# Eight gate projections of a hybrid attention/SSD block: placed between the attention heads, with the gates kept in DRAM

## The chip, the cores and the metric

One core of a Trainium2 chip runs the whole program. The metric is device time in microseconds of one execution, as the median of several. TensorE (PE in the rows) multiplies matrices, VectorE (DVE) and ScalarE (ACT) work on elements, GpSimd (POOL) does a few powers, and SyncE (SP) issues nearly all DMA transfers.

## What is computed

One encoder block with two parallel branches over 16 learned rows and 512 input rows, width 1024, in float32:

```python
u = rmsnorm(h, norm_w)
proj = u @ w_in                      # latents, rope key, gate of attention, SSD z/x/B/C/dt, merge gates
y_a = mla_branch(q_lat, kv_lat, k_rope, ...)          # 16 heads
y_a = (y_a * silu(g_attn)) @ w_attn_proj
y_s = ssd_branch(z, xbc, dt_raw, ...) @ w_ssd_proj    # chunked scan, both directions, 4 groups
gates = sigmoid(merge).reshape(B, L, 2, 1024)
mixed = gates[:, :, 0] * y_a + gates[:, :, 1] * y_s
h = rmsnorm(h + mixed @ w_out, final_norm_w)
```

The change concerns `gates[:, :, 0]`, the output gate of the attention branch: eight blocks of 128 columns, each a projection of `u` (contraction 1024, 512 rows).

## The kernel before

**Arithmetic.** Every projection is done as three passes of float32r matmuls: the operands are split into a high and a low part, and high x high, high x low and low x high are summed in PSUM. A projection of 128 output columns over 512 rows is therefore 24 matmuls (8 blocks of the contraction, 3 passes). Its weights come in as one 512 KB load into `wr` (2 buffers); ScalarE casts the high part `wh` and VectorE subtracts to get the low part `wl` (3 buffers each), `weights`, lines 492 to 516.

**Stages.** First the norm of the input, then four groups of the SSD branch, each with its projections, and from about 500 us the 16 attention heads. A head is `score_gen` (four score tiles in two double-bank PSUM buffers, tag "d"; maximum on VectorE, exponential on ScalarE, normalisation) and `value_gen` (five rounds: TensorE transposes the probabilities, ScalarE and VectorE split them into `pT`, TensorE multiplies them with the values into `o`). Each pair of heads p needs projections `q_unit(p)`, `k_unit(p)`, `g_fill(p)` (the silu gate, 24 matmuls), every second pair `pe_unit` and `v_unit`. After head 15, `split_y` makes the high and low parts `yah`, `yal` of the attention output, `mix_unit(m)` for eight blocks m projects them with `w_attn_proj`, multiplies with the gate and adds the SSD part, and `out_unit` multiplies with `w_out` (tile `wo`), followed by residual and norm.

**The merge gates.** `merge_s(m)` (lines 1268 to 1278) makes the gate of the SSD branch and applies it to `ysacc` at once. `merge_a(m)` (lines 1283 to 1292) makes tanh of half the projection for the attention branch: 24 matmuls, then one ScalarE activation into a tile `ma`. That tile stays in the pool of slots until `mix_unit(m)` uses it (lines 1303 to 1319).

**Room.** One pool of `NSLOT` = 31 slots of 128 x 512 float32 holds nearly all working tiles: the latents, the values, the small weights `ws` of the heads, the heads' outputs, the gates, and at the end `yah`, `yal` (16 slots) and `mxh`, `mxl` (up to 16). PSUM has 4 single banks, tag "m", for projections, transposes and `o`.

**The order.** Nothing runs in the order in which it is written. `drive` (lines 1441 to 1460) steps through generators with a clock of its own: the `mains` (the heads, the SSD stages) and a `queue` of fillers, of which the first 20 (`LOOK`) are looked at and up to 4 (`OPEN`) are under way at a time; each has a condition on what is done. A main item that is ready goes before a filler. What is recorded so gets a rank, and `_Recorder.order` (lines 164 to 255) then lists all operations by the earliest time at which a cost table says they can go, ties by rank, on every engine and on SP. An operation that is the first to use a pool's tile may overtake at most 4 (`AHEAD`) older tiles of the same pool. The sorted list is emitted; each engine keeps its part of it.

The fillers around the change, in the queue's order for each pair p: `pe_unit`, `q_unit`, `k_unit`, `v_unit`, `merge_s(p)`, `g_fill(p + 1)` (lines 1525 to 1535). Behind all pairs come the eight `merge_a`, with one condition for all: head 13 (`GATES`) is done (line 1536). `mix_unit` is admitted when all eight `split_y` are done (line 1545).

Of the kernel before, what the change touches and what calls it, by code (L numbers as in the profile page):

```python
# [9 lines left out]
F32 = mybir.dt.float32  # L10
# [6 lines left out]
P = 128  # L17
D = 1024
NM = 16
NX = 512  # L20
# [5 lines left out]
KD = D // P  # L26
NC = NX // P
EPS = 1e-6
NH = 16
# [14 lines left out]
LAG = 1250.0  # L44
MAHEAD, TOKC, CBC = 2, 2, 1
MAINS, OPEN, LOOK = 24, 4, 20
QLATE, GATES, SPLIT = 1, 13, 99


WPOOL, WPOOLB = 2, 4  # L50
# [2 lines left out]
class _Plan:  # L53
# [7 lines left out]
    @staticmethod  # L61
    def region(ap):
        step = ap.ap[0][0]
        p0, f0 = divmod(ap.offset, step) if step else (0, ap.offset)
        span = sum(abs(st) * (n - 1) for st, n in ap.ap[1:]) + 1
        return ap.name, p0, p0 + ap.shape[0], f0, f0 + span
# [25 lines left out]
class _Recorder:  # L92
# [15 lines left out]
    @classmethod  # L108
    def region(cls, ap):
        step = ap.ap[0][0]  # L110
        if ap.name == "cum_rows":
            return 0, 1, [(0, 1)]
        p0, f0 = divmod(ap.offset, step) if step else (0, ap.offset)
        dims = [(st, n) for st, n in ap.ap[1:] if st and n > 1]
        if "PSUM" in str(getattr(ap, "space", "")):
            end = f0 + sum(st * (n - 1) for st, n in dims)
            return 0, P, [(f0 // cls.BANK * cls.BANK, (end // cls.BANK + 1) * cls.BANK)]
        dims.sort(reverse=True)
        spans = [(f0, f0 + 1)]
        for k, (st, n) in enumerate(dims):  # L120
            rest = sum(a * (b - 1) for a, b in dims[k:]) + 1
            inner = sum(a * (b - 1) for a, b in dims[k + 1:]) + 1
            if inner >= st or n * len(spans) > 32:
                return p0, p0 + ap.shape[0], [(a, a + rest) for a, _ in spans]
            spans = [(a + st * m, a + st * m + 1) for a, _ in spans for m in range(n)]
        return p0, p0 + ap.shape[0], spans
# [227 lines left out]
def hybrid_block_kernel(ctx, tc, a, out):  # L354
    nc = tc.nc
    scr = nc.dram_tensor("cum_rows", (2, NC, 32, P), F32, kind="Internal").ap()

    cp = ctx.enter_context(tc.tile_pool(name="cp", bufs=1))
    rp = ctx.enter_context(tc.tile_pool(name="rp", bufs=WRAW))
# [12 lines left out]
    def nm(s):  # L372
        uid[0] += 1
        return f"{s}_{uid[0]}"

    def slot(shape, dt=F32, name="s"):
        return rec.tile(sp.tile(shape, dt, tag="s", name=nm(name)), "s", NSLOT)
# [15 lines left out]
    def bank(tag, shape, name, wait=lambda: True):  # L393

        yield lambda: wait() and bool(banks[tag]) and done.look(min(banks[tag]))
        banks[tag].remove(min(banks[tag]))
        return (psm if tag == "m" else psd)(shape, name=name)

    def drop(tag):
        banks[tag].append(plan.unit_end)  # L400
# [17 lines left out]
    done = Done()  # L418
# [5 lines left out]
    V, A, G, T = (_Eng(plan, rec, n, e) for n, e in (("DVE", nc.vector), ("ACT", nc.scalar), ("POOL", nc.gpsimd), ("PE", nc.tensor)))  # L424
    S, Q = _Queue(plan, rec, nc.sync), _Queue(plan, rec, nc.scalar, "ACT")
# [4 lines left out]
    def tt(eng, o, x, y, op):  # L430
        eng.tensor_tensor(o, x, y, op=op)

    def lo_of(eng, lo, x, hi):
        eng.tensor_tensor(lo, x, hi.bitcast(F32), op=ALU.subtract)

    def mm(o, lhs, rhs, start=True, stop=True):
        T.matmul(o, lhsT=lhs, rhs=rhs, start=start, stop=stop)
# [54 lines left out]
    def weights(srcs, k, c, small=False):  # L492
        after = 0.0
        if small:
            raw = slot([P, k, c], name="ws")
        else:
            after = min(raws)
            raws.remove(after)
            raw = rec.tile(rp.tile([P, k, c], F32, tag="wr", name=nm("wr")), "rpwr", WRAW)
        for dst, src in srcs(raw):  # L500
            S.dma_start(dst, src, after)
        yield
        if small:
            hi, lo = slot([P, k, c], F32R, name="wsh"), slot([P, k, c], F32R, name="wsl")
        else:
            yield lambda: bool(splits) and done.look(min(splits))
            splits.remove(min(splits))
            hi = rec.tile(wp.tile([P, k, c], F32R, tag="wh", name=nm("wh")), "wpwh", WSPLIT)
            lo = rec.tile(wp.tile([P, k, c], F32R, tag="wl", name=nm("wl")), "wpwl", WSPLIT)
        wcount[0] += 1  # L510
        A.copy(hi, raw)
        lo_of(V, lo, raw, hi)
        if not small:
            raws.append(plan.unit_end)
        yield
        return hi, lo

    def wdone():
        splits.append(plan.clk["PE"] + 100.0)

    def w_cols(c0, M=P):
        return weights(lambda raw: [(raw, w_in[:, :, c0:c0 + M])], KD, M)
# [3 lines left out]
    def proj(w, src, cols, M=P, tag="m", width=HALF):  # L526


        hi, lo = w
        n = len(src)  # L530
        parts = [cols] if tag == "m" else cols
        ps = yield from bank(tag, [P, 512] if tag == "m" else [P, 2, 512], "pj", lambda: not mid[0])
        seq = [(hi, 0, k) for k in range(n)] + [(lo, 0, k) for k in range(n)] + [(hi, 1, k) for k in range(n)]
        for h, s in list(enumerate(parts))[::-1]:
            o = ps[:M, :cols.stop - cols.start] if tag == "m" else ps[:M, h, :width]
            for i, (x, y, k) in enumerate(seq):
                mm(o, x[:, k, :], src[k][y][:, s], start=(i == 0), stop=(i == len(seq) - 1))
                mid[0] = h > 0 or i < len(seq) - 1
                if i % (PART * len(parts)) == PART * len(parts) - 1 and mid[0]:
                    yield  # L540
        return o if tag == "m" else ps[:M, :, :width]
# [256 lines left out]
    def has(*keys):  # L798
        return lambda: all(k in done for k in keys)
# [318 lines left out]
    def score_ok(h):  # L1118
        return h < 0 or ("S", h) in done
# [148 lines left out]
    def merge_s(m):  # L1268
        w = yield from w_cols(O_MS + m * P)
        ps = yield from proj(w, u_src, QRY)  # L1270
        wdone()
        yield
        z = slot([P, NX], name="ms")
        A.activation(z, ps, AF.Tanh, scale=0.5)
        drop("m")
        yield
        V.scalar_tensor_tensor(ysacc[:, m, :], z, 1.0, ysacc[:, m, :], op0=ALU.add, op1=ALU.mult)
        done.add(("ms", m))

    w_ap = a["w_attn_proj"][0].rearrange("(k p) m -> p k m", p=P)  # L1280
    mx_, gates, ysp = {}, {}, {}

    def merge_a(m):
        w = yield from w_cols(O_MA + m * P)
        ps = yield from proj(w, u_src, QRY)
        wdone()
        yield
        z = slot([P, NX], name="ma")
        A.activation(z, ps, AF.Tanh, scale=0.5)
        drop("m")  # L1290
        gates[m] = z
        done.add(("ga", m))

    def split_y(p):
# [7 lines left out]

    def mix_unit(m):
        w = yield from weights(lambda raw: [(raw, w_ap[:, :, m * P:(m + 1) * P])], KD, P)
        ps = yield from proj(w, [ysp[p] for p in range(KD)], slice(0, NX))
        wdone()
        yield has(("ga", m), ("ms", m))
        z = gates.pop(m)
        V.scalar_tensor_tensor(z, z, 1.0, ps, op0=ALU.add, op1=ALU.mult)
        drop("m")  # L1310
        tt(V, z, z, ysacc[:, m, :], ALU.add)
        yield
        h = slot([P, NX], F32R, name="mxh")
        l = slot([P, NX], F32R, name="mxl")
        A.copy(h, z)
        yield
        lo_of(V, l, z, h)
        mx_[m] = (h, l)
        done.add(("mx", m))
# [117 lines left out]
    def fill(makes, cond=None):  # L1437
        for mk in makes:
            queue.append(Item(mk, cond))
# [31 lines left out]
    def proj_fill(g):  # L1471
        fill([mark(lambda m=m: proj_unit(g, m), ("proj", g, m)) for m in range(4)], lambda: epi_ok(g))
# [52 lines left out]
    for p in range(KD):  # L1525
        if p % 2 == 0:
            fill([lambda p=p: pe_unit(p // 2)], lambda p=p: lat_ok() and score_ok(2 * p - 3))
        fill([lambda p=p: q_unit(p), lambda p=p: k_unit(p)], lambda p=p: "att" in done and lat_ok() and score_ok(2 * p - 2))
        if p % 2 == 0:
            fill([lambda p=p: v_unit(p // 2)], lambda p=p: lat_ok() and (p == 0 or ("A", 2 * p - 3) in done))  # L1530
        if p == 0:
            proj_fill(3)
        fill([lambda p=p: merge_s(p)], lambda p=p: ("proj", 3, p // 2) in done)
        if p + 1 < KD:
            g_fill(p + 1)
    fill([lambda m=m: merge_a(m) for m in range(KD)], lambda: ("A", GATES) in done)
    for h in range(NH):
        main(lambda h=h: score_gen(h), lambda h=h: ("q", h) in done and ("k", h) in done
             and (h < 1 or ("P", h - 1) in done) and (h < 2 or ("A", h - 2) in done))
# [47 lines left out]
```

## Time and profile before

| | |
|---|---|
| median of 3 runs | 912.46 us (910.71 to 915.15) |
| the profiled execution, its own time | 913.33 us |
| its span, first to last instruction | 911.5 us |
| TensorE busy | 878.5 us (96%) |
| VectorE busy | 707.9 us (78%) |
| ScalarE busy | 543.2 us (60%) |
| granted TensorE clock, mean | 0.996 |
| DMA | 83.30 MB, 91 GB/s |

"Busy" is the union of an engine's records. A record of a matmul lasts from its start to its modelled end (about 0.39 us for 512 columns), while the next one starts 0.23 us later, so that short stalls do not show as idle time. Row formats: `out<-in` names the tiles written and read, `x` is a count, and in brackets stands idle time of the engine just ahead of the instruction with what ended it. All operations are recorded at line 261, where the sorted list is emitted, so the rows are told apart by tile names: `pj<-uh,wh` (and `wl`, `ul`) is a projection of `u` in 512-column matmuls, `pj<-nh,wsh` one of the latents, `sc` the scores, `pt` the transposes, `o` the value products, `v` the values, `pj<-yah,wh` a mix projection, `wo` the output.

### The profile page before, as it was taken

What the parts mean: (1) busy time and instruction counts of PE and PEld (TensorE: products, weight loads), DVE (VectorE), ACT (ScalarE), POOL (GpSimd) and SP (SyncE); (2) the same over time, 40 slices, a digit from 0 to 9 for tenths busy, and PEclk for the clock granted to TensorE, in tenths of its full rate; (3) what the DMA queues carried; (4) which work ended last, traced back from release to release, by engine and by line L of the source; (5) the groups of instructions that cost most, each with busy time, mean ns of one, the idle gap of its engine ahead of it and who ended that gap; (6) DMA issues with size and microseconds to landing.
All of it is one profiled execution on the core that took longest, in us unless ns stands there. A gap on an engine that the chain in (4) does not pass through costs nothing.

```text
span 911.5 us, 13243 instructions
## 1 busy us (share of the span) xinstructions
PE 878.5 (96%) x4984; PEld 725.7 (80%) x4984; DVE 707.9 (78%) x1245; ACT 543.2 (60%) x1159; POOL 11.7 (1%) x20
## 2 busy tenths in 40 slices
PE   7999999999989999999999999999999999999997
PEld 5997878867878769977788888877777878888885
DVE  6798799968799689979768757969989897334464
ACT  6369469965776447855344556757777685432232
POOL 1000000000000000000001000000000000000000
PEclk9999999999999999999999999999999999999998
DMA  7254246434524236332224333121121001433322
GB/s 219 71 165 119 70 120 166 109 93 113 141 70 139 70 84 160 104 116 70 70 70 102 81 87 92 38 53 29 38 50 33 15 24 47 135 121 101 104 70 92
DMA packets 126952, 83.30 MB, mean 91 GB/s; under 512 B 26354, under 2 KB 114071, under 8 KB 126889
## 3 DMA queue, kind: packets, MB, share of 16 engines
q1 hardware_dynamic: 126709, 82.33, 33.3%
q8 instruction: 39, 0.64, 0.3%
q14 instruction: 24, 0.20, 0.1%
q10 hardware_dynamic: 180, 0.14, 0.0%
HBM read 80.22 MB, written 2.23 MB: 90 GB/s over the span
## 4 chain that ended last, share of the span: by engine, by line
PE 74%; DVE 17%; ACT 4%; issue 2%; DMA 1%; POOL 0%; POOLq 0%; ACTq 0%; DVEq 0%
PE pj L261 53%; PE wo L261 4%; PE sc L261 3%; PE st L261 2%; PE yo L261 2%; PE o L261 2%; DVE x L261 2%; DVE wl L261 2%; PE pt L261 2%; PE tr L261 2%; PE yd L261 1%; DVE mx L261 1%; DVE pT L261 1%; DVE yo L261 1%; DVE C L261 1%
## 5 line engine op out<-in xcount | busy, mean ns | idle before, releaser
L261 PE MATMUL pj<-uh,wh 128*128 128x512 f32 (+3 forms) x776 | 158.8, 346 | 8.0 <-DVE yo L261 3.5
L261 DVE TENSOR_TENSOR wl<-wr,wh 128x1024 fp32r<-128x1024 f32 (+1 forms) x102 | 123.9, 1217 | 53.2 <-ACT wh L261 53.0
L261 PE MATMUL pj<-uh,wl 128*128 128x270 f32 (+3 forms) x776 | 157.1, 339 | 0.0
L261 PE MATMUL pj<-ul,wh 128*128 128x270 f32 (+3 forms) x776 | 150.0, 335 | 0.0
L261 ACT CAST wh<-wr 128x1024 fp32r<-128x1024 f32 (+1 forms) x102 | 106.3, 1042 | 63.1 <-PE pj L261 41.3
L261 PEld LDWEIGHTS pj<-uh,wh 128*128 128x128 f32 (+1 forms) x776 | 121.9, 191 | 27.6 <-issue 5.1
L261 PEld LDWEIGHTS pj<-ul,wh 128*128 128x128 f32 (+1 forms) x776 | 122.6, 189 | 15.0
L261 PEld LDWEIGHTS pj<-uh,wl 128*128 128x128 f32 (+1 forms) x776 | 122.0, 190 | 13.2 <-issue 0.2
L261 ACT ACTIVATE ar<-ar,nacs 128x128 f32<-128x128 f32 x256 | 80.8, 391 | 24.5 <-DMA ar<-cum_rows 19.3
L261 PE MATMUL sc<-kst,qst 96*128 96x264 f32 (+1 forms) x384 | 67.2, 299 | 6.3 <-ACT p L261 5.4
L261 PEld LDWEIGHTS sc<-kst,qst 96*128 96x128 f32 (+1 forms) x384 | 53.6, 189 | 11.7 <-ACT p L261 8.6
L261 ACT ACTIVATE p<-sc,mx 128x528 f32<-128x528 f32 x64 | 45.3, 707 | 21.3 <-DVE mx L261 20.8
L261 PE MATMUL pt<-cst,p 128*128 128x128 f32 (+1 forms) x320 | 52.2, 274 | 1.4 <-DVE pT L261 0.8
L261 DVE TENSOR_TENSOR pT<-pt,pT 128x512 fp32r<-128x512 f32 x64 | 43.8, 685 | 11.5 <-ACT pT L261 11.3
L261 PE MATMUL o<-pT,v 128*128 128x512 f32 x128 | 46.6, 417 | 3.5 <-ACT pT L261 2.9
L261 DVE SCALAR_TENSOR_TENSOR x<-pj,chv,x 128x528 f32<-128x528 f32 x64 | 48.8, 763 | 0.8 <-ACT x L261 0.3
L261 PEld LDWEIGHTS pt<-cst,p 128*128 128x128 f32 (+1 forms) x320 | 37.3, 130 | 12.7 <-DVE p L261 1.5
L261 DVE TENSOR_REDUCE mx<-sc 128x1 f32<-128x528 f32 x64 | 44.6, 698 | 2.2 <-PE sc L261 1.9
L261 ACT CAST pT<-pt 128x512 fp32r<-128x512 f32 x64 | 37.3, 587 | 14.6 <-PE pt L261 14.4
L261 ACT ACTIVATE w<-cbm,dt_t 128x128 f32<-128x128 f32 x128 | 39.9, 390 | 2.9 <-DVE cbm L261 2.9
L261 PE MATMUL pj<-nh,wh 128*128 128x512 f32 x128 | 39.6, 431 | 0.0
L261 DVE SCALAR_TENSOR_TENSOR w<-cbm,dt_t,w 128x128 f32<-128x128 f32 x128 | 38.1, 347 | 0.0
(224 smaller groups left out, 1467.2 us busy)
## 6 DMA issues: line engine op xcount, KB each, us to landing
wr<-in_w_in SPq DMA_DIRECT2D x69, 512.0 KB, 4.0
ar<-cum_rows SPq DMA_DIRECT2D x32, 512.0 KB, 5.3
wr<-in_w_ssd_proj SPq DMA_DIRECT2D x16, 512.0 KB, 3.4
wr<-in_w_attn_proj SPq DMA_DIRECT2D x8, 512.0 KB, 3.6
wr<-in_w_out SPq DMA_DIRECT2D x8, 512.0 KB, 3.7
ws<-in_w_uq SPq DMA_DIRECT2D x36, 64.0 KB, 3.3
xt<-in_x SPq DMA_DIRECT2D x4, 512.0 KB, 5.3
fin<-in_x SPq DMA_DIRECT2D x4, 512.0 KB, 6.0
```

What stands on the lines that cost most here:

```text
L261: o.fn(*o.args, **o.kw)
```

## The change

`merge_a(m)` no longer keeps its tile for the mix: it stores the 256 KB of tanh to a DRAM tensor `gate_rows`, and `mix_unit(m)` loads them into a new slot, after its weights and ahead of its projection. The queue has `merge_a(p - 1)` right behind `merge_s(p)`, admitted when head 2p - 1 is done (for p = 1 to 7), and `merge_a(7)` behind all pairs, admitted when head 14 is done. The recorder treats each block of the new tensor as a region of its own, so that a load depends on its own store alone. The arithmetic is the same.

```diff
-QLATE, GATES, SPLIT = 1, 13, 99
+QLATE, SPLIT = 1, 99
@@
             return 0, 1, [(0, 1)]
+        if ap.name == "gate_rows":
+            return 0, 1, [(ap.offset // (P * NX), ap.offset // (P * NX) + 1)]
@@
     scr = nc.dram_tensor("cum_rows", (2, NC, 32, P), F32, kind="Internal").ap()
+    gate_scr = nc.dram_tensor("gate_rows", (KD, P, NX), F32, kind="Internal").ap()
@@
-    mx_, gates, ysp = {}, {}, {}
+    mx_, ysp = {}, {}
@@ def merge_a(m):
         z = slot([P, NX], name="ma")
         A.activation(z, ps, AF.Tanh, scale=0.5)
         drop("m")
-        gates[m] = z
+        yield
+        S.dma_start(gate_scr[m], z)
         done.add(("ga", m))
@@ def mix_unit(m):
         w = yield from weights(lambda raw: [(raw, w_ap[:, :, m * P:(m + 1) * P])], KD, P)
+        yield has(("ga", m))
+        z = slot([P, NX], name="ga")
+        S.dma_start(z, gate_scr[m])
         ps = yield from proj(w, [ysp[p] for p in range(KD)], slice(0, NX))
         wdone()
-        yield has(("ga", m), ("ms", m))
-        z = gates.pop(m)
+        yield has(("ms", m))
         V.scalar_tensor_tensor(z, z, 1.0, ps, op0=ALU.add, op1=ALU.mult)
@@
         fill([lambda p=p: merge_s(p)], lambda p=p: ("proj", 3, p // 2) in done)
+        if p:
+            fill([lambda p=p: merge_a(p - 1)], lambda p=p: ("A", 2 * p - 1) in done)
         if p + 1 < KD:
             g_fill(p + 1)
-    fill([lambda m=m: merge_a(m) for m in range(KD)], lambda: ("A", GATES) in done)
+    fill([lambda: merge_a(KD - 1)], lambda: ("A", NH - 2) in done)
```

## Rows read from the trace of the kernel before

**Rows 1.** The page: busy time of each engine.
```profile
PE 878.5 (96%) x4984; PEld 725.7 (80%) x4984; DVE 707.9 (78%) x1245; ACT 543.2 (60%) x1159; POOL 11.7 (1%) x20
```
**Rows 2.** Busy us of each engine (instructions in brackets), and granted clock, in four stretches.
```profile
core 0: us, PE busy (x) PEld busy (x) DVE busy (x) ACT busy (x) POOL busy (x), PEclk, DMA share, GB/s
...
615.70:762.80 147.10, 137.45 (x835) 114.78 (x835) 131.02 (x267) 109.00 (x234) 0.00 (x0) 1.00 0.14 32
763.40:815.80 52.40, 52.40 (x254) 42.97 (x253) 23.22 (x33) 21.60 (x36) 0.00 (x0) 1.00 0.39 118
815.80:877.00 61.20, 61.20 (x266) 49.60 (x265) 26.42 (x32) 16.29 (x19) 0.00 (x0) 1.00 0.28 88
577.70:615.70 38.00, 37.23 (x230) 31.66 (x228) 29.42 (x61) 24.77 (x56) 0.00 (x0) 1.00 0.25 58
```
**Rows 3.** TensorE's timeline among the gates: start, duration, matmuls in a run.
```profile
768.21 0.60 PE L261 MATMUL pt<-cst,p 128*128 128x128 f32 x4
768.57 2.08 PE L261 MATMUL pj<-uh,wh 128*128 128x512 f32 x8
...
780.20 0.89 PE L261 MATMUL sc<-kst,qst 128*128 128x264 f32 x6
780.93 1.08 PE L261 MATMUL pj<-uh,wl 128*128 128x512 f32 x4
...
804.65 2.02 PE L261 MATMUL pj<-uh,wh 128*128 128x512 f32 x8
806.51 2.01 PE L261 MATMUL pj<-uh,wl 128*128 128x512 f32 x8
```
**Rows 4.** TensorE's groups by shape, 615.7 to 762.8 us: first and last.
```profile
L261 PE MATMUL o<-pT,v 128*128 128x512 f32 x80 | 30.3, 421 | 3.3 <-ACT pT L261 2.9 <-DVE pT L261 0.4
...
L261 PE MATMUL v<-wsh,nl 128*16 128x256 f32 x4 | 0.8, 278 | 0.0
```
**Rows 5.** TensorE's groups by shape, 577.7 to 615.7 us: first and last.
```profile
L261 PE MATMUL pt<-cst,p 128*128 128x128 f32 x39 | 6.5, 275 | 0.3 <-DVE p L261 0.3
...
L261 PE MATMUL v<-wsh,nh 128*16 128x256 f32 x2 | 0.4, 279 | 0.0
```
**Rows 6.** TensorE's groups by shape, 763.4 to 815.8 us: first and third.
```profile
L261 PE MATMUL pj<-uh,wl 128*128 128x512 f32 x64 | 17.3, 398 | 0.0
...
L261 PE MATMUL pj<-uh,wh 128*128 128x512 f32 x56 | 14.4, 398 | 0.0
```
**Rows 7.** Who waited for whom from 560 us on: total us, times, longest.
```profile
PEld sc L261 <- ACT p L261: 8.6, 13, 1.7
...
PEld o L261 <- ACT pT L261: 3.6, 3, 1.3
```
**Rows 8.** Tile `ma`, the gates: duration ns min/median/max, first and last start us.
```profile
L261 ACT ACTIVATE ma<-pj x8: 578/598/602, 767.9 to 816.0; 128x512 f32<-128x512 f32 x8
L261 DVE SCALAR_TENSOR_TENSOR ma<-ma,pj x8: 681/689/689, 821.5 to 877.2; 128x512 f32<-128x512 f32 x8
```
**Rows 9.** Tile `wh`, 577 to 816 us: the two parts of a block of weights.
```profile
L261 ACT CAST wh<-wr x15: 1037/1049/1067, 580.0 to 810.9; 128x1024 fp32r<-128x1024 f32 x15
L261 DVE TENSOR_TENSOR wl<-wr,wh x15: 1209/1225/1227, 586.2 to 812.0; 128x1024 fp32r<-128x1024 f32 x15
```
**Rows 10.** DMA issues from 560 us on: count, size, median us to landing.
```profile
out<-fo SPq DMA_DIRECT2D x8, 256.0 KB, 2.2
...
fw<-in_final_norm_w SPq DMA_DIRECT2D x2, 256.0 KB, 4.3
```
**Rows 11.** VectorE's timeline: output sums of heads 13 and 15, and the last split.
```profile
763.57 0.69 DVE L261 TENSOR_TENSOR y<-o,y 64x512 f32<-64x512 f32 x1
...
806.99 0.69 DVE L261 TENSOR_TENSOR y<-o,y 64x512 f32<-64x512 f32 x1
...
809.09 0.69 DVE L261 TENSOR_TENSOR yal<-y,yah 128x512 fp32r<-128x512 f32 x1 [0.69 <-ACT yah L261]
```
**Rows 12.** Busy us by engine in the last stretch, columns as in rows 2.
```profile
900.00:920.00 20.00, 4.73 (x21) 3.52 (x19) 5.32 (x11) 4.29 (x9) 1.66 (x3) 0.83 0.27 105
```

## The prediction

> **What bounds the kernel now.** I read the page first: TensorE is busy 96% of the span, VectorE 78%, ScalarE 60% [rows 1]. So TensorE's work sets the time wherever it is full, and the change removes none of that work. What can be won or lost is TensorE's stalls, and I looked for them by stretch [rows 2]. From 577.7 to 615.7 us (the pair of heads 2 and 3) and from 615.7 to 762.8 us (five pairs, heads 4 to 13) TensorE is seen idle for 0.8 and 9.7 us; from 763.4 to 815.8 us (the rest of heads 14 and 15, with the gates) and from 815.8 to 877.0 us (mixes) never. In the five pairs VectorE is busy 131.0 of 147.1 us, 89%; among the gates only 23.2 of 52.4 us, 44%. That is the picture to see: a stretch of heads in which the chain score, maximum, exponential, transposition, split, product keeps TensorE waiting [rows 7], and behind it a stretch of plain projections in which VectorE and ScalarE have little to do.
>
> Visible idle time understates the stalls, since a matmul's record lasts longer than its step. So I sum steps. From the starts of runs that follow each other without a wait, 512 columns take 1.86/8 = 0.232 us, scores of 264 columns 0.73/6 = 0.122 us, transposes of 128 columns 0.36/4 = 0.090 us [rows 3]. The five pairs hold 835 matmuls [rows 2], in 21 groups by shape [rows 4], which add up to 280 of 512 columns, 357 of 256 or 264 and 198 of 128: 65.0 + 43.6 + 17.8 = 126.4 us of steps. Stalls: 147.1 - 126.4 = 20.7 us, 4.1 us in a pair of 29.4 us. The pair of heads 2 and 3, by the same sum over 230 matmuls [rows 2, 5]: 81 x 0.232 + 102 x 0.122 + 47 x 0.090 = 35.4 us, stalls 2.6 of 38.0 us. It is special in that 54 of its 81 long matmuls belong to projections of u, more than two units of 24; a later pair has one such unit (its silu gate), 127 in five pairs. The stretch with the gates holds 254 matmuls [rows 2], of which 184 belong to gates (three groups of 64, 64 and 56) [rows 6]: 202 x 0.232 + 16 x 0.122 + 36 x 0.090 = 52.1 us, stalls 0.3 of 52.4 us. So the more projections lie among the heads, the fewer stalls are left.
>
> **What the change does, part by part.** *The move.* Seven gates, each 24 x 0.232 = 5.6 us of TensorE's steps, become fillers between pairs; six of them (blocks 0 to 5) fall among the heads up to head 13, one into each of the pairs of rows 2. A pair then has 25.3 + 5.6 = 30.9 us of TensorE's work and two units to fill with, as the pair of heads 2 and 3 had. I take that pair's rate: 2.6 x 30.9/35.4 = 2.3 us of stalls instead of 4.1, for five pairs 5 x 1.85 = 9.3 us gained. The pair of heads 2 and 3 I leave as it is. The best end is the rate of the stretch with the gates, 0.3 in 52: nearly all of 20.7 + 2.6 us goes, about 22. The worst end is below nothing: with each unit come one high and one low part of weights, 1.05 us on ScalarE and 1.23 us on VectorE [rows 9], and a tanh of 0.60 us [rows 8]. If the chain over VectorE, not TensorE, set a pair's time, six units would add 6 x 1.23 = 7.4 us and fill nothing. Against that end: VectorE's 131.0/5 = 26.2 us for a pair become 27.4, below TensorE's 30.9, and ScalarE's 21.8 become 23.4. I take 9.3 because the pair with the same mixture is in the trace.
>
> A side effect comes from the queue: the waiting gates take places among the 20 fillers that are looked at, so the last one or two `merge_s` are admitted a pair or so later. Their work moves from ahead of the heads into the pairs, which is more filling; I cost it at nothing.
>
> *The closing stretch.* Between the output of head 13 and the end of the last split (763.6 to 809.8 us) the gates were the cover for heads 14 and 15 [rows 11]. TensorE's own work there is 52.1 - 184 x 0.232 = 9.4 us; with the two gates that remain (6 and 7), 20.5 us. What has to pass in this time is the remaining score tiles, the two value stages, and the tail from the sum of head 15 to the last split, 809.8 - 807.0 = 2.8 us [rows 11]. VectorE's load is small: 23.2 us less about six low parts, 23.2 - 7.4 = 15.8 us [rows 2, 9]. So TensorE still has the larger sum, and I take stalls at the rate above, 20.5 x 2.6/35.4 = 1.5 us instead of 0.3: a loss of 1.2 us. Ends: 0, and the first rival's 13.
>
> *Stores and loads.* Eight stores and eight loads of 256 KB are added, 4 MB to 83. Nearest rows of that size: a store lands in 2.2 us, a load in 4.3 us [rows 10]. The DMA share in the four stretches is 0.14 to 0.39 [rows 2], so the wires are no bound. A store waits on SP for its tanh; behind it are queued the next `wr` and `ws` loads, and behind these ScalarE's and VectorE's splits. The order is sorted by planned times, so the wait is only by how much the tanh is late; bounds 0 and, for a store in each pair, some 0.6 us (one tanh) x 8 = 5 us, and only where the load behind it is late for its use. I take 0. The load of a gate is issued after its block's weights and ahead of a projection of 5.6 us, which covers 4.3 us; what is late waits on VectorE with its PSUM bank held, while three other banks go on. If the cover is gone it is the last block that counts, at most 4.3 us once; I take 0.
>
> *Room.* The eight gates held eight slots from 767.9 us until their use at 821.5 to 877.2 us [rows 8]; now each holds one for a tanh and a store, about 3 us, and one again from its load. During the mixes TensorE was never idle before [rows 2], so room that comes free gains nothing there, and the loads must not take more than came free. The last load may have to wait for a slot until the last projection frees `yah`; the output products of the other blocks lie in between. I take 0.
>
> *Sum.* -9.3 + 1.2 = -8.1 us against the profiled execution of 913.33 us (span 911.5 us and 1.8 us around it): 905.2 us. The median of the runs lies 0.87 us below that execution, so 904.4, rounded to 904 us.
>
> **The rivals.** *A, slower: the closing stretch loses its cover.* If gates 6 and 7 are spent while head 14 is under way, the last head runs alone. Head 13 to head 15 at the pace of a pair (29.4 us) plus 2.8 us and the split is about 33 us against 20.5 us of TensorE's work: 13 us lost instead of 1.2. With the pairs at half the gain (4.7 us) that is 912.5 - 4.7 + 13 = 921 us; it decides from the point at which the loss exceeds the pairs' gain. For it: the chain of the last head can't be shortened. Against it: heads 14 and 15 need no projections of their own, and first matmuls of several mixes can run before the last split.
>
> The clock was granted in full in all four stretches [rows 2] and read 0.83 only in the last one, in which TensorE was busy 4.7 us [rows 12]. The Trainium skill (TensorE: Matmul & The Clock Gate, Part 1) says that the array's default is half the clock and that activity releases it; this speaks against the change, since it takes the cover off TensorE ahead of the mixes. By that rule rival A would also run about one mix projection of 24 matmuls at 1.2 GHz, an estimate of 5.6 us more, so 926 us; in the forecast, with stalls of 1 us and less as in the trace, it would change nothing, and the clock of 1.00 in the pairs agrees.
>
> *B, no change: the holes aren't where the filler lies.* The order on each engine is fixed beforehand, so a gate's 24 matmuls help only where the plan put them; stalls of a few tenths of a us, waits of TensorE for the exponential and for `pT` [rows 7], may stay between them. Gain 0 to 4 us, loss 1.2: 910 to 914 us. For it: the heads' silu gates are such fillers already, and 4.1 us a pair are left.
>
> *C, more: the pairs come near to the rate of the stretch with gates.* 22 us less 1.2: 891.5 us.
>
> *D, it doesn't do what it says.* The condition on a gate gives it a rank, not a place. If the sorting puts the gates late all the same, the stretches stay as they are, with 16 more transfers: 912 to 913 us.
>
> **How the numbers follow.** Forecast (gain 5 to 16, loss 0 to 4, so 896 to 908) 0.50; C 0.14; B 0.20; A with the worst end of VectorE 0.11; D 0.05. A run can tell about 0.5% (4.6 us) from no change. Faster by more: the forecast, C and a seventh of B, 0.67. Within 0.5%: the rest of B and D, 0.22. Slower: 0.11. The range goes from C's 892 to 914 us; it leaves out A and the far half of C.
>
> **What would show it.** Right: the gates' activations spread over the heads from about 590 us on; pairs of 33 us instead of 29.4, with stalls of 2 to 3 us by the sum of steps; the mixes beginning about 8 us earlier than 815.8 us; VectorE's share in the pairs falling from 89% to about 83%. Wrong: a visible gap of TensorE between head 15 and the first mix (A); idle rows for the exponential and `pT` as long as before (B); gates still behind 767 us (D); VectorE waiting for the loaded gates, or SP's queue behind a store.

## The result and the profile after

| | before | after |
|---|---|---|
| median | 912.48 us (910.71 to 915.15) | 901.72 us (899.13 to 903.12) |
| ratio | | 0.9876, 95% interval 0.9843 to 0.9909 |
| profiled execution, its span | 913.33, 911.5 us | 903.12, 901.3 us |

The change made the kernel 1.2% faster, 10.8 us. 904 us was predicted, 892 to 914 as the range.

TensorE's work is what it was; the page's row on the engines, for [rows 1]:

```profile
PE 877.8 (97%) x4984; PEld 727.1 (81%) x4984; DVE 709.5 (79%) x1245; ACT 544.3 (60%) x1159; POOL 11.7 (1%) x20
```

The gates and their transfers, from the tiles `ma` and `gate_rows` of the changed kernel (duration in ns, first and last start in us), for [rows 8, 10]:

```profile
L263 ACT ACTIVATE ma<-pj x8: 587/597/598, 583.1 to 800.4; 128x512 f32<-128x512 f32 x8
...
L263 SPq DMA_DIRECT2D gate_rows<-ma x8: 320/339/344, 583.7 to 801.0; - x8
L263 SPq DMA_DIRECT2D ga<-gate_rows x8: 338/441/831, 792.6 to 862.6; - x8
```

So the gates do lie among the heads, from 583 us on instead of 768. Next the stretches that answer to [rows 2], cut at the same events in both kernels: from the output sum of head 1 to that of head 13, from there to the end of the last split, and the mixes. First before, then after (busy us of each engine and instructions, clock, DMA):

```profile
577.70:763.60 185.90, 175.47 (x1067) 147.08 (x1066) 161.13 (x330) 134.52 (x291) 0.00 (x0) 1.00 0.16 37
763.60:809.80 46.20, 46.20 (x228) 37.97 (x227) 21.82 (x31) 19.89 (x33) 0.00 (x0) 1.00 0.41 125
```

```profile
579.30:783.70 204.40, 202.78 (x1199) 171.78 (x1198) 168.55 (x332) 143.58 (x298) 0.00 (x0) 1.00 0.23 62
783.70:809.20 25.50, 24.21 (x130) 19.15 (x129) 17.15 (x29) 14.45 (x27) 0.00 (x0) 1.00 0.46 154
...
809.20:863.60 54.40, 54.40 (x237) 44.03 (x236) 23.81 (x30) 13.83 (x16) 0.00 (x0) 1.00 0.33 107
```

Between head 1 and head 13 TensorE's visible idle time fell from 10.4 to 1.6 us, although the stretch holds 132 more matmuls. By the prediction's sum of steps, with each matmul counted where it starts: before, 362 matmuls of 512 columns, 458 of 256 or 264 and 244 of 128 make 161.8 us of steps in 185.8 us, **24.0 us of stalls**; after, 513, 447 and 236 make 194.8 us in 204.4 us, **9.6 us**. By pairs of heads, before 3.7, 3.7, 4.9, 2.6, 5.4 and 3.7 us; after 1.7, 1.0, 1.6, 1.2, 1.3 and 2.8 us. Before, these stalls stood around the output sums of the odd heads: from 4 us ahead to 3 us behind these six sums there are 12.5 us, around the six of the even heads 2.9 us; after, 1.9 and 1.8 us. VectorE's share fell from 87% to 82% of the stretch. The closing stretch shrank from 46.2 to 25.5 us since 1.6 units of 24 matmuls lie in it instead of 6.5, and its stalls rose from 0.4 to **2.9 us**; the visible gap is 1.3 us where there was none. In the mixes nothing changed: TensorE is never idle in either kernel.

TensorE's waits for the exponential and for `pT`, for [rows 7], both kernels from 577 to 810 us, first before, then after:

```profile
PEld sc L261 <- ACT p L261: 7.0, 12, 1.2
...
PEld o L261 <- ACT pT L261: 3.6, 3, 1.3
```

```profile
PEld sc L263 <- ACT p L263: 1.4, 5, 0.3
...
PEld o L263 <- ACT pT L263: 0.2, 1, 0.2
```

**One thing in the two profiled executions is not the change.** Around 482 us, in the same part of the program, the executions differ in the clock (columns as above; the changed kernel, the kernel before, and the changed kernel once more, from the run e9 below, which is 3.5 us earlier at this place):

```profile
482.00:490.00 8.00, 7.77 (x25) 5.85 (x25) 4.49 (x10) 1.99 (x7) 2.50 (x3) 0.59 0.56 131
```

```profile
482.00:490.00 8.00, 7.77 (x38) 5.97 (x37) 6.91 (x13) 4.12 (x8) 2.39 (x3) 1.00 0.57 131
```

```profile
478.50:486.50 8.00, 7.77 (x38) 5.97 (x38) 6.64 (x13) 4.12 (x11) 2.50 (x3) 1.00 0.55 131
```

In the changed kernel's profiled execution the clock was at 0.59 there, and 25 matmuls ran in the time of 38. From 478 to 505 us this execution has 4.2 us of stalls by steps at the full clock, the one of before 0.9 us. The account of the two profiled executions is therefore -14.4 us among the heads, +2.5 us at the close, +3.3 us by this clock, and -1.9 us from 505 us to head 1 (2.8 us of stalls before, 0.9 after): -10.5 us against -10.2 us between the spans; up to 478 us the stalls differ by 0.3 us, behind the last split by 0.1 us. The clock and the SSD stages vary by some us from execution to execution (the output sum of head 1 is at 579.3 us in this execution and at 572.9 us in e9's, of the same kernel), so the experiments are judged first by their heads, from head 1 on.

### The profile page after: what moved, and what is told of

The parts are those of the page before. It is cut to its first block, busy times and chain, and to the rows that moved or that the text cites. A ratio compares the mean times of both kernels' runs of the same rounds, so it can differ in the third digit from the quotient of the medians.

```text
span 901.3 us, 13280 instructions
## 1 busy us (share of the span) xinstructions
PE 877.8 (97%) x4984; PEld 727.1 (81%) x4984; DVE 709.5 (79%) x1245; ACT 544.3 (60%) x1159; POOL 11.7 (1%) x20
## 4 chain that ended last, share of the span: by engine, by line
PE 77%; DVE 14%; ACT 4%; issue 2%; DMA 1%; POOL 0%; POOLq 0%; SPq 0%; ACTq 0%; DVEq 0%
PE pj L263 53%; PE wo L263 4%; PE sc L263 4%; PE pt L263 3%; PE o L263 2%; PE st L263 2%; PE yo L263 2%; DVE wl L263 2%; DVE x L263 2%; PE tr L263 2%; PE yd L263 1%; DMA ar<-cum_rows 1%; PE v L263 1%; DVE yo L263 1%; ACT p L263 1%
## 5 line engine op out<-in xcount | busy, mean ns | idle before, releaser
L263 PE MATMUL pj<-uh,wh 128*128 128x512 f32 (+3 forms) x776 | 162.6, 348 | 7.7 <-DVE yo L263 3.2
L263 PE MATMUL sc<-kst,qst 96*128 96x264 f32 (+1 forms) x384 | 65.0, 297 | 0.7 <-DVE kst L263 0.3
L263 ACT ACTIVATE p<-sc,mx 128x528 f32<-128x528 f32 x64 | 45.0, 703 | 27.5 <-DVE mx L263 26.4
L263 PE MATMUL o<-pT,v 128*128 128x512 f32 x128 | 44.5, 405 | 0.4 <-DVE pT L263 0.4
```

The costliest lines, as they stand in the source:

```text
L263: o.fn(*o.args, **o.kw)
```

## The experiments

Theory: the gain is in the filling. A unit of 24 matmuls lying at the right places among the heads takes off stalls; the DRAM trip costs nothing by itself and is needed only for room. Rivals: the freed slots make the gain; VectorE's load sets the pairs' time; the trip's waits take part of it back; the moved `merge_s` make it; only the number of units counts and not their place.

What was measured, all by the same sums (stalls of TensorE in us; "heads" from the output sum of head 1 to that of head 13, "close" from there to the last split). Each ratio is to the kernel before, run on the same chip; the chips differ, so ratios are compared and not medians:

| kernel | median us | ratio to before, 95% interval | heads: us, stalls | close: us, stalls |
|---|---|---|---|---|
| before | 912.5 | | 185.8, 24.0 | 46.2, 0.4 |
| after | 901.7 | 0.9876 (0.9843 to 0.9909) | 204.4, 9.6 | 25.5, 2.9 |
| e1 through DRAM, behind | 912.9 | 0.9987 (0.9975 to 0.9998) | 185.8, 23.9 | 46.2, 0.4 |
| e2 between, in slots | 913.8 | 1.0005 (0.9991 to 1.0020) | 209.1, 18.2 | 32.3, 4.1 |
| e3 four between, four behind | 904.3 | 0.9888 (0.9871 to 0.9904) | 199.8, 15.7 | 35.7, 2.4 |
| e4 no gates | 876.3 | 0.9583 (0.9568 to 0.9598) | 185.9, 24.9 | 17.8, 6.0 |
| e5 no low parts of the gates | 901.4 | 0.9861 (0.9841 to 0.9880) | 206.0, 10.6 | 25.8, 3.9 |
| e6 no trip | 899.5 | 0.9848 (0.9830 to 0.9866) | 204.5, 9.7 | 25.5, 2.9 |
| e7 28 fillers looked at | 900.1 | 0.9845 (0.9827 to 0.9864) | 199.4, 10.2 | 25.5, 2.9 |
| e8 last gate later | 902.4 | 0.9872 (0.9853 to 0.9890) | 204.4, 9.7 | 23.0, 4.8 |
| e9 after, once more | 900.4 | 0.9848 (0.9823 to 0.9872) | 204.3, 9.5 | 25.5, 2.9 |
| e10 at even heads | 918.4 | 1.0055 (1.0042 to 1.0068) | 221.5, 25.5 | 23.0, 4.9 |
| e11 28 slots | 906.1 | 0.9922 (0.9907 to 0.9937) | 210.1, 15.4 | 25.5, 2.9 |
| e12 places exchanged | 901.2 | 0.9872 (0.9851 to 0.9894) | 202.3, 10.1 | 24.6, 2.8 |

In two of these stretches the clock fell, and the sum counts that as stalls: among the heads of e10 and at the close of e8. Both are given below with their price.

Run e9, for the size of what can be told apart:

> The changed kernel itself, beside the next two and against the kernel before on this chip. Every theory: 0.9876 of the kernel before, within 0.003.

Its ratio lies 0.0028 below the first one, inside that interval; its stalls agree to 0.1 us. Differences of 0.3% between the kernels of the table are not told from none by their times.

### Place or store: e1, e2, e11

e1, against the changed kernel:

```diff
-        if p:
-            fill([lambda p=p: merge_a(p - 1)], lambda p=p: ("A", 2 * p - 1) in done)
...
-    fill([lambda: merge_a(KD - 1)], lambda: ("A", NH - 2) in done)
+    fill([lambda m=m: merge_a(m) for m in range(KD)], lambda: ("A", 13) in done)
```

> The changed kernel with its stores and loads, but the eight gates behind the heads as before (one condition for all: head 13 is done). Theory (the place between the heads makes the gain, the DRAM trip by itself is free): the time of the kernel before, 912.5 us, within 4 us, with stalls of about 20 us in the five pairs again and the mixes beginning at about 816 us. Rival 1 (eight slots that come free let the heads run on): 5 to 10 us faster than before. Rival 2 (the trip costs, since SP waits on the activations): 4 us or more slower than before.

1.2 us below the kernel before (0.9987), and pair by pair its stalls to 0.1 us. Store and load alone are worth 0 to 2 us; the gain is in the place.

e2, against the changed kernel:

```diff
-        S.dma_start(gate_scr[m], z)
+        gates[m] = z
...
-        yield has(("ga", m))
-        z = slot([P, NX], name="ga")
-        S.dma_start(z, gate_scr[m])
...
-        if p:
+        if p > 1:
             fill([lambda p=p: merge_a(p - 1)], lambda p=p: ("A", 2 * p - 1) in done)
...
-    fill([lambda: merge_a(KD - 1)], lambda: ("A", NH - 2) in done)
+    fill([lambda m=m: merge_a(m) for m in [*range(1), 7]], lambda: ("A", 13) in done)
```

> No DRAM tensor: gates 1 to 6 between the heads under the same conditions as in the changed kernel, kept in slots until the mix as before; gates 0 and 7 behind head 13. Theory (filling is what counts; the DRAM trip is only there for room): if room suffices, six units still fill, 8 to 10 us faster than before, 902 to 905 us. Rival (slots held for up to 200 us delay the small weights and the values of the heads): the stalls move to waits on slots and the time is that of before or above, 910 to 925 us.

The time is the rival's: no gain. Gates 0 and 7 lie behind head 13 here, so six gates are held among the heads. The loss is not all among them: the heads of the profiled execution still have 5.8 us of stalls less than before, but the close has 3.7 us more, the stretch from 505 us to head 1 has 2.0 us more, and the clock fell at 482 us. The pairs up to head 9 look much as after (2.9, 0.7, 1.4 and 1.5 us of stalls), but the pair of heads 10 and 11 has 8.1 us:

```profile
717.70:759.00 41.30, 37.25 (x216) 30.31 (x215) 30.26 (x64) 25.68 (x57) 0.00 (x0) 1.00 0.15 37
```

Among TensorE's waits there are those ahead of the values of the next heads (its timeline in that kernel):

```profile
729.37 0.51 PE L263 MATMUL v<-wsh,nh 128*128 128x256 f32 x2 [0.52 <-ACT wsh L263]
...
732.65 0.51 PE L263 MATMUL v<-wsh,nh 128*128 128x256 f32 x2 [0.58 <-DVE pT L263]
...
748.09 0.51 PE L263 MATMUL v<-wsh,nh 128*128 128x256 f32 x2 [0.42 <-DVE v L263]
```

`v_unit` needs slots for its weights and for five value tiles. That these slots came late is argued and not seen: its rounds are spread over 24 us here and over 22 us in the changed kernel too. To take the slots alone, e11 is the changed kernel with fewer of them:

```diff
-NSLOT = 31
+NSLOT = 28
```

> The changed kernel with 28 slots in the pool instead of 31: as if three gates were held, with nothing else of the order's rules changed. Theory (with the gates kept in slots the gain was lost since the small weights and the values of the heads waited for slots): the stalls between head 1 and head 13 rise from 9.6 us to 15 us or more, the mixes too get room late, and the time rises by 5 us or more, to 907 us and above (the SSD stages before may lose time as well, so the stretch of the heads is to be compared). Rival (the loss of that kernel came from its other place for gates 0 and 7): the stretch of the heads keeps 9 to 11 us of stalls.

The heads' stalls rose to 15.4 us, and nearly all of it, 6.3 us instead of 1.3, is in that same pair of heads 10 and 11, with two of the same waits:

```profile
728.91 0.51 PE L263 MATMUL v<-wsh,nh 128*128 128x256 f32 x2 [0.52 <-ACT wsh L263]
...
732.19 0.50 PE L263 MATMUL v<-wsh,nh 128*128 128x256 f32 x2 [0.59 <-DVE pT L263]
```

So three slots fewer, with no gate moved, make most of the hole that six held gates make. Room is what the DRAM trip buys. The close, at 2.9 us, did not get worse, and about half of the gain is left (0.9922): the rest of what e2 lost came with its other places for gates 0 and 7 or with the longer holding, which no run separates.

### How much, and where: e3, e10, e12

e3, against the changed kernel:

```diff
-        if p:
+        if 0 < p <= 4:
             fill([lambda p=p: merge_a(p - 1)], lambda p=p: ("A", 2 * p - 1) in done)
...
-    fill([lambda: merge_a(KD - 1)], lambda: ("A", NH - 2) in done)
+    fill([lambda m=m: merge_a(m) for m in range(4, KD)], lambda: ("A", 13) in done)
```

> The changed kernel with gates 0 to 3 between the heads and gates 4 to 7 behind head 13, all through DRAM. Theory (each unit between heads takes off 2 to 2.5 us of stalls; with four gates behind, the closing stretch keeps its cover): a gain of four units, about 9 us, and none of the 2.5 us lost in the closing stretch: 902 to 906 us, the last two or three pairs with 4 us of stalls each, the closing stretch with 0.5 us. Rival (cover of the close matters more than the filling): faster than the changed kernel, under 900 us.

The time came as expected. The four pairs with a gate have 1.6, 1.1, 2.0 and 1.9 us of stalls, the two without 5.4 and 3.7 us, as before. The expectation on the close was wrong: with more than three units of cover it still had 2.4 us. The units were used up before the end, and the gap ahead of the last value products, where `pT` is awaited (0.87 us), stayed.

e10, against the changed kernel:

```diff
-            fill([lambda p=p: merge_a(p - 1)], lambda p=p: ("A", 2 * p - 1) in done)
+            fill([lambda p=p: merge_a(p - 1)], lambda p=p: ("A", 2 * p - 2) in done)
```

> The changed kernel with gate p - 1 admitted when head 2p - 2 is done, one head earlier than head 2p - 1; the silu gate of a later pair is admitted at an even head too, so that both units of a pair come together. Theory of the place (the kernel before stalled at the ends of the odd heads, where its silu gate was used up, and the gates fill just these holes): the stalls there come back in part, 2.5 to 3.5 us in a pair instead of 1.3, and the time rises by 5 to 10 us, 907 to 912 us. Rival (only the number of units in a pair counts, the sort puts their matmuls where TensorE is free): 902 us within 2 us.

One head earlier, and the kernel is slower than before: 918.4 us, 16 to 18 us above the changed kernel. The heads have as many units and 25.5 us of stalls. TensorE's timeline from 695 to 740 us shows why; first this kernel's runs of projections of u, then the changed kernel's:

```profile
697.02 0.51 PE L263 MATMUL o<-last,v 128*128 128x512 f32 x1 [0.57 <-DVE last L263]
699.19 0.47 PE L263 MATMUL o<-pT,v 128*128 128x512 f32 x1 [1.01 <-DVE y L263]
...
710.65 2.02 PE L263 MATMUL pj<-uh,wh 128*128 128x512 f32 x8
...
714.38 2.02 PE L263 MATMUL pj<-ul,wh 128*128 128x512 f32 x8
...
717.39 2.03 PE L263 MATMUL pj<-uh,wh 128*128 128x512 f32 x8
...
722.03 2.02 PE L263 MATMUL pj<-ul,wh 128*128 128x512 f32 x8
...
734.37 0.51 PE L263 MATMUL sc<-kst,qst 128*128 128x264 f32 x2 [0.77 <-ACT p L263]
```

```profile
703.88 2.02 PE L263 MATMUL pj<-uh,wh 128*128 128x512 f32 x8
...
708.01 2.01 PE L263 MATMUL pj<-ul,wh 128*128 128x512 f32 x8
...
716.76 0.64 PE L263 MATMUL pj<-uh,wh 128*128 128x512 f32 x2
717.27 0.71 PE L263 MATMUL pj<-uh,wh 128*128 128x512 f32 x2
718.05 0.86 PE L263 MATMUL pj<-uh,wh 128*128 128x512 f32 x3
...
722.10 2.01 PE L263 MATMUL pj<-ul,wh 128*128 128x512 f32 x8
```

In e10 the two units of a pair run one behind the other from 710.7 to 724 us, and there are waits on both sides. In the changed kernel they lie apart, and the first eight matmuls of the second are cut into pieces of one to three between other work. Counted by the output sums, 12 to 19 of a pair's matmuls of `u` lie ahead of the sum of its even head in the changed kernel; in e10 it is none to two, and 11 in the last pair. Around the odd heads' sums e10 has 15.2 us of stalls, around the even ones 3.4 us, as before the change.

Up to 1.8 us of the 25.5 us are the clock, which fell in the pair of heads 6 and 7 behind waits of TensorE (the matmuls that started at the lower clock have 1.8 us of steps at the full one):

```profile
663.00:667.00 4.00, 4.00 (x20) 3.77 (x21) 2.85 (x10) 1.63 (x5) 0.00 (x0) 0.62 0.02 6
```

The verdict does not hang on that.

e12 exchanges the two, against e10:

```diff
-             lambda: p < 2 or ("A", 2 * p - 2) in done)
+             lambda: p < 2 or ("A", 2 * p - 1) in done)
```

(the condition in `g_fill`).

> As the kernel with the gates at even heads, with the silu gate of pair p now admitted when head 2p - 1 is done, one head later than before: the two fillers of a pair come at one head's end each again, but in exchanged places. Theory (a unit at every head's end is what fills; two units together leave the next 15 us without any): the two runs of 24 matmuls of a pair lie apart again, stalls of 1.5 to 2.5 us in a pair, 9 to 13 us between heads 1 and 13, and the time of the changed kernel, 898 to 905 us. Rival (the merge gates have to lie at the odd heads, where the next pair's scores wait for q and k): stalls of 3.5 us and more in a pair, 910 us or above.

The gain is back, 0.9872 and 10.1 us of stalls. Which of the units lies at which head does not matter; that one of them comes at each head's end does. Both units at the odd heads were not tried.

### What a unit brings along: e4, e5, e6, e7

e4, against the kernel before:

```diff
-        yield has(("ga", m), ("ms", m))
-        z = gates.pop(m)
-        V.scalar_tensor_tensor(z, z, 1.0, ps, op0=ALU.add, op1=ALU.mult)
+        yield has(("ms", m))
+        z = slot([P, NX], name="ga")
+        V.scalar_tensor_tensor(z, ysacc[:, m, :], 1.0, ps, op0=ALU.add, op1=ALU.mult)
...
-    fill([lambda m=m: merge_a(m) for m in range(KD)], lambda: ("A", GATES) in done)
```

> The kernel before without the eight gate projections, their weights and activations; the mix uses the other gate's sum in their place. It measures what the gates cost as a whole. Their steps on TensorE are 8 x 24 x 0.232 = 44.5 us. Theory (in the kernel before they hid nothing but the closing of heads 14 and 15, in the changed kernel they also fill about 14 us of stalls): 872 to 878 us, that is 35 to 40 us below before and 24 to 30 us below the changed kernel, with 20 us of stalls in the five pairs and 5 to 10 us of stalls between head 13 and the last split. Rival (no cover was needed at the close): 868 us, the full 44.5 us below before.

The gates cost 37.8 us on this chip in the kernel before; by the first ratio, 0.9876 of 914.1 us, 26.4 us in the changed kernel. Their steps are 44.5 us. With no cover at all the close has 6.0 us of stalls, far from the 13 us that rival A put on it.

e5, against the changed kernel (`low=False` for the gates alone):

```diff
...
-        lo_of(V, lo, raw, hi)
+        if low:
+            lo_of(V, lo, raw, hi)
...
```

> The changed kernel without the low part of the gates' weights: VectorE's subtraction of 1.2 us is left out for the eight gates, and the high part stands in its place in the matmuls, so that TensorE's work stays as it is. It takes 8 x 1.23 = 9.8 us off VectorE, 7.4 us of them in the pairs of heads. Theory (TensorE sets the pairs' time, VectorE has room once a second unit fills): the time of the changed kernel, 902 us, within 2 us. Rival (VectorE's chain sets the pairs' time, so each unit's low part is paid): 5 to 8 us faster than the changed kernel, 894 to 897 us.

9.8 us less for VectorE, and 901.4 us: nothing. VectorE's low parts do not set the pairs' time.

e6, against the changed kernel:

```diff
-        S.dma_start(gate_scr[m], z)
...
-        S.dma_start(z, gate_scr[m])
...
-        V.scalar_tensor_tensor(z, z, 1.0, ps, op0=ALU.add, op1=ALU.mult)
+        V.scalar_tensor_tensor(z, ysacc[:, m, :], 1.0, ps, op0=ALU.add, op1=ALU.mult)
```

> The changed kernel without the eight stores and eight loads; the gates are computed in the same places and thrown away, and the mix multiplies with the other gate's sum. SP no longer waits for the activations (61.6 us in all in the changed kernel, up to 10.7 us at a time). Theory (what SP waits for is hidden, the weights are loaded long ahead): the time of the changed kernel, 902 us, within 2 us. Rival (weights queued behind a waiting store come late): 3 to 6 us faster.

899.5 us, and the stalls of the changed kernel to 0.1 us in every pair. The trip costs no more than can be told. SP's row in the changed kernel (505 us to the end) shows long waits all the same:

```profile
SPq L263 <- ACT ma L263: 61.6, 8, 10.7
```

They are hidden: without them the time is the same. That what stands behind the store in the queue is not due yet is the likely reason, and argued.

e7, against the changed kernel:

```diff
-MAINS, OPEN, LOOK = 24, 4, 20
+MAINS, OPEN, LOOK = 24, 4, 28
```

> The changed kernel with 28 fillers looked at instead of 20, so that the waiting gates keep no merge_s out. In the changed kernel merge_s 5 to 7 came at 568.8, 613.6 and 647.9 us, in the kernel before at 558.1, 579.1 and 600.8 us. Theory (part of the gain is these units' moving into the pairs: stalls between 505 and 579 us fell from 2.8 to 0.9 us): the units come back to the front and the time rises by 1 to 3 us, 903 to 905 us. Rival (the side effect costs and gains nothing): 902 us within 1 us.

The three `merge_s` came back to 558.4, 572.2 and 583.0 us, and the time did not rise: 0.9845 beside e9's 0.9848. My theory for these units fell; the stalls between 505 us and head 1 stayed at 0.8 us without them. Why that stretch has 1.9 us less than before stays open.

### The close: e8

```diff
-    fill([lambda: merge_a(KD - 1)], lambda: ("A", NH - 2) in done)
+    fill([lambda: merge_a(KD - 1)], lambda: ("A", NH - 1) in done)
```

> The changed kernel with the last gate admitted when head 15 is done instead of head 14, so that it lies behind the last head's products as cover for the copies and splits that end the heads. Theory (the closing stretch lost its cover: 2.9 us of stalls between head 13 and the last split instead of 0.4, of which 1.5 us stand in two gaps behind the last products): the mixes' first matmuls find all splits done, the stretch has 1 to 1.5 us of stalls, and the time falls by 1 to 2 us against the changed kernel, 900 to 901 us. Rival (the unit is then missing between heads 14 and 15): the stalls move there and the time stays at 902 us or rises by 1 us.

The time is the rival's, 902.4 us, with 4.8 us of stalls instead of 2.9: the tail behind the last products is covered, and the stalls stand among head 15's rounds. How much of them is the missing unit stays open, since the clock fell just there in this execution, behind 4 us in which TensorE was busy for 3.1:

```profile
788.00:792.00 4.00, 3.08 (x20) 2.13 (x17) 3.94 (x9) 2.21 (x6) 0.00 (x0) 1.00 0.67 202
792.00:796.00 4.00, 3.42 (x14) 2.32 (x14) 2.59 (x6) 2.88 (x5) 0.00 (x0) 0.67 0.51 194
```

The matmuls that started at the lower clock have 1.5 us of steps at the full one, which is most of the 1.9 us more. No kernel here that computes and uses the gates beats the changed one by more than the intervals.

## Why the prediction was right, point by point

- **TensorE's stalls among the heads are what can be won**: right, e1 and e4 have them unchanged and the changed kernel lost 14.4 of 24.0 us.
- **The rate of the pair of heads 2 and 3** as what is left (2.3 us in a pair, 9.3 us gained): too small a gain, on a ground that does not hold. Four of the five later pairs have 1.0 to 1.6 us left and only the last has 2.8; the pair of heads 2 and 3, which I left as it was, went from 3.7 to 1.7 us as well. The term of -9.3 us measured -14.4 us. The 2.6 us that I took for this pair come from where I let the stretch end, at 615.7 us: that is 0.8 us ahead of head 3's output sum, and just behind it TensorE waited 0.98 us:

```profile
615.69 0.44 PE L261 MATMUL pt<-cst,p 128*128 128x128 f32 x2
617.11 0.88 PE L261 MATMUL sc<-kst,qst 128*128 128x264 f32 x5 [0.98 <-ACT p L261]
```

Taken from output sum to output sum the pair had 3.7 us, hardly less than the 4.1 us of a later pair, although it held 52 matmuls of `u` and a later pair 24 or 34; only 8 of the 52 lay ahead of head 2's sum. So the step that more projections leave fewer stalls did not show in that pair, and e10 shows it wrong as it stands: it has the changed kernel's number of units and 25.5 us of stalls. I named the fixed order as rival B, but did not see that the two units have to lie a head apart, though the stalls before stood at the ends of the odd heads.
- **Luck in the number**: with 3.7 us the same sum gives some 4 us gained among the heads, 1.9 us lost at the close, and 910 us (an estimate). The short stretch, which erred in its favour, and the place of the units, which the sum does not hold, brought 904 us as near as it is.
- **The worst end, VectorE's chain** (+7.4 us): right to be set aside, e5.
- **The side effect on `merge_s`, costed at nothing**: right, e7.
- **The close**, +1.2 us: it measured +2.5 us. The rate of a pair did not hold there. The larger of TensorE's two gaps stands ahead of the last value products, where only `pT` is awaited and the gates are used up, the smaller one behind them:

```profile
803.85 0.50 PE L263 MATMUL pj<-yah,wh 128*128 128x512 f32 x1 [0.88 <-DVE pT L263]
...
808.52 0.50 PE L263 MATMUL pj<-yah,wh 128*128 128x512 f32 x1 [0.24 <-ACT yah L263]
```

Rival A's 13 us was too much, as e4's 6.0 us without any cover shows.
- **Stores**: the cost of 0 was right, e6; the bound on the wait (0.6 us a store) was not, SP waited up to 10.7 us, at no price (e6).
- **Loads**: hidden, as said. The two of the eight whose landing the trace holds took 4.0 and 5.6 us in place of the 4.3 us of [rows 10], and VectorE waited 18.7 us ahead of their use, all of it for TensorE's projection:

```profile
L263 DVE SCALAR_TENSOR_TENSOR ga<-ga,pj x8: 679/688/689, 812.8 to 867.2; 128x512 f32<-128x512 f32 x8
...
  PE pj L263: 18.7, 8
...
DMA to landing us min/median/max: 4.0/4.8/5.6
```

- **Room gains nothing**: right for the mixes and for slots that come free (e1), but the prediction gave the trip no worth. With the gates held in slots there was no gain (e2), and three slots fewer took about half of it (e11).
- **The sum**: -8.1 us predicted, -10.8 us measured by the medians. With its two terms as they came out, -14.4 and +2.5 us, it is -11.9 us; what lies between this and the two profiled executions' -10.2 us is the clock at 482 us (+3.3) and the stretch ahead of head 1 (-1.9).
- **The clock**: in the two kernels it fell in none of the heads' stretches and not at the close, where TensorE's gaps were 1.3 us in all, so the rule that was weighed did not decide. It can come in: in e8 the clock did fall at the close (0.67 from 792 to 796 us), and in e4, with no gates there at all, it did not.

## What to carry to other kernels

Where one stage is bound by a chain and the next is plain matmul work without dependences, put the units of the second between the steps of the first, and look at which step's end each falls: two units at one end left the other ends empty and lost all that was won. Measure the stalls by steps, not by busy time, per repetition of the stage, and let every repetition begin and end at the same event. A result that is done early has to wait somewhere; if the pool is tight, 256 KB to DRAM and back cost nothing that could be measured here, while three slots fewer cost 5 to 6 us (e11 beside e9, on one chip).

## What the hardware showed

The clock fell in the middle of the program in some executions, and not in others of the same kernel. In the changed kernel's profiled execution the fall follows 2 us in which TensorE ran 18 one-column matmuls (`ssq`). TensorE's timeline of the changed kernel, then of the kernel before:

```profile
480.00 2.06 PE L263 MATMUL ssq<-ones,sq 128*128 128x1 f32 x18
481.92 1.17 PE L263 MATMUL pj<-nh,wh 128*128 128x512 f32 x4
...
486.27 1.91 PE L263 MATMUL pj<-nl,wh 128*128 128x512 f32 x4
```

```profile
479.65 2.06 PE L261 MATMUL ssq<-ones,sq 128*128 128x1 f32 x18
481.58 1.17 PE L261 MATMUL pj<-nh,wh 128*128 128x512 f32 x4
...
484.75 1.09 PE L261 MATMUL pj<-nl,wh 128*128 128x512 f32 x4
```

The same four matmuls took 1.91 us in the one and 1.09 us in the other. In the windows' row from 484 to 488 us the changed kernel's clock is 0.50, the lower of the two levels:

```profile
484.00:488.00 4.00, 4.00 (x13) 2.84 (x12) 2.21 (x4) 0.63 (x1) 0.73 (x1) 0.50 0.82 163
```

TensorE counts as busy for all of those 4 us, so only the clock's column and the steps show it. The Trainium skill (TensorE: Matmul & The Clock Gate, Part 1) has the clock follow how busy the array is. These rows do not settle that: matmuls of one column had gone before in the changed kernel, but the kernel before ran the same 18 and kept 1.00. From 478 to 505 us the profiled executions of the kernel before, e1, e7, e8, e9, e10, e11 and e12 have 0.9 to 1.1 us of stalls; those of after, e2, e3, e4, e5 and e6 have 2.6 to 4.2 us. A fall around 270 us stands in 12 of the 14 profiled executions, all but those of the kernel before and e6; the changed kernel's:

```profile
266.00:276.00 10.00, 7.79 (x33) 6.75 (x34) 10.00 (x16) 6.56 (x16) 0.00 (x0) 0.66 0.29 77
```

What decides these falls was not tried.
